# Twelve pairs instead of eight in the first pass of the up products, a new order for two operand sums, and another buffer for one product of the last rows

## The chip, the cores and the metric

The kernel runs on one core of one Trainium2 chip. The metric is the device time of the whole program in microseconds (us). Below, PE is the matrix engine (TensorE), DVE the vector engine, ACT the scalar engine, POOL is GpSimd, and SP is the engine that issues most transfers.

## The reference

A trunk of two layers over 1024 tokens of width 1024, all in float32. Every sub-layer is `h = h + post_norm(sublayer(pre_norm(h)))`. Layer 0 mixes tokens by latent attention, layer 1 by a gated linear recurrence (HGRN2); each is followed by an MLP with 4096 hidden features:

```python
def sq_relu_mlp(h, w1, w2):
    a = jax.nn.relu(h @ w1)
    return (a * a) @ w2

def rms_norm(x, g):
    xf = x.astype(jnp.float32)
    y = xf * lax.rsqrt(jnp.mean(xf * xf, axis=-1, keepdims=True) + EPS)
    return (y * g.astype(jnp.float32)).astype(x.dtype)
```

The change touches the first product of each MLP, `h @ w1` (the up products), and the last normalisation of layer 1's MLP, which ends the kernel.

## The kernel before

**Products in three matmuls.** A float32 operand is split into a high part, rounded by ACT, and a low part, the rest, by DVE (`split`, lines 76 and 77). `mm3` (lines 81 to 83) then makes each product from three matmuls. So every operand, weight or activation, costs one ACT and one DVE instruction before PE can use it, and the split of 128 x 1024 numbers is the common unit.

**Strassen's scheme in the MLP.** The activations A (features by tokens) are seen as 2 x 2 blocks `B11`, `B12`, `B21`, `B22`: the first index halves the features, the second the tokens. B11 and B21 hold the first 512 tokens, B12 (stored whole, unsplit) and B22 the last 512. The weights `w1` are taken in 16 pairs of 128-column blocks (`NP`, the pair's number is `p`). Seven products per pair replace eight. Each product is 12 matmuls of 128 x 512 columns (four feature tiles by three, in `product`), so a pair is 84 matmuls. The right-hand operands are B11, B21, B22 and four sums of blocks, T1 to T4:

- `tsums12` makes T1 and T2, `tsums34` makes T3 and T4. Each T is made in two halves of 128 x 1024 by DVE additions and subtractions and then a split. The temporaries come from the four tiles of tag `s`; the two that `tsums12` leaves in `t2s` are read again for T4.
- All four T need the last rows of tokens. B11 and B21 don't.

**First pass.** For the pairs `p < EARLY` the two products that need only the first 512 tokens are made ahead of everything else, two pairs at a time: `raw_early` loads the pair's first 128 columns (512 KB), `w_parts` splits them, `first_two` multiplies by B11 and ACT copies the sum into `sP1` (line 814), POOL sends `sP1` to `psp` in HBM (line 879), `add_second` adds the product with B21, and ACT makes squared ReLU `h11` of it (lines 806 and 807), which `spill` sends to `hsp` (line 803). `sP1` and `h11` of the first pass live in a ring of two tiles, tag `he`. This pass fills PE while the last token rows are still being normalised, transposed (`into_features`, lines 176 to 181) and summed into T1 to T4. Its instructions are traced with a priority 150 places ahead of their own (`AHEAD`); the transposes of the rows stand 150 (layer 0) or 250 places (layer 1) behind theirs (`LAG`).

**Main pass.** For every pair, `raw_half` loads the pair's two halves of weights (`rA`, `rB`, 512 KB each) into three raw tiles in turn. For `p < EARLY`, `h11` and `sP1` are read back from HBM (lines 894 and 896, SP's queue) and `others` makes the remaining five products. For later pairs all seven products are made there. `others` makes the weight sums `s12` (lines 826, 827) and `s34` (832, 833), splits them (`wS12`, `wS34`), and multiplies: b = wS12 x T2, c = wS12 x T1, d = wS34 x T3, then c += wS34 x B22 and d += wb x T4. DVE adds `U = b + sP1` (837), `X5 = c + U` (844), then `h22`, `h12`, `h21` (848, 851, 854); c gets its second product only after X5 has read it. Four more sums (859 to 869) and seven spills follow.

**What sets the order.** The program is traced in the order of the code, and a list scheduler then fixes each engine's order of instructions at compile time: by priority (place in the trace, shifted as above) among what is ready in its own estimate of times. The tiles of a ring are given out when free. The engines run their fixed orders and wait on semaphores.

**The end of the kernel.** In layer 1's `mlp_down`, `done(t)` finishes each of the last four row tiles: DVE adds the last product (line 1103), ACT squares the sum for the mean (line 135), DVE multiplies the same tile by the gain in place (1105), adds the two means (144), POOL takes the power -0.5 (145), DVE scales and adds the residual (1109), SP stores. `U[t]` is a tile of the same shape whose values are no longer needed there.

Of the kernel before, what the change touches and what calls it, by code (L numbers as in the profile page):

```python
# [16 lines left out]
ALU = mybir.AluOpType  # L17
# [19 lines left out]
ROPE_BASE = 10000.0  # L37
LAG = (150, 100, 250)
AHEAD = (150, 150)
EARLY = 8  # L40
SCALE = (NOPE + ROPE) ** -0.5


# [15 lines left out]
def trunk(ctx, tc, x, x_t, positions, norm_gains, mla_w_in, mla_q_norm, mla_kv_norm, mla_w_uq, mla_w_ukv, mla_w_o,  # L59
          hgrn_w_in, hgrn_lb_logits, hgrn_o_norm, hgrn_w_o, mlp_w1, mlp_w2, out):  # L60
    nc = tc.nc
    PE, ACT, DVE, POOL, SP = nc.tensor, nc.scalar, nc.vector, nc.gpsimd, nc.sync
# [6 lines left out]
    def new(p, shape, dt, tag, bufs=None):  # L69
        uid[0] += 1  # L70
        kw = {} if bufs is None else {"bufs": bufs}
        return p.tile(shape, dt, tag=tag, name=f"{tag}_{uid[0]}", **kw)

    def split(dst, src):

        ACT.activation(dst[:, 0], src, AF.Copy)  # L76
        DVE.tensor_tensor(dst[:, 1], src, dst[:, 0].bitcast(F32), ALU.subtract)  # L77
# [587 lines left out]
    with qstack:  # L665
        with tc.tile_pool(name="mla_wo", bufs=1, side="left", reuse_waits="tile") as wp:
            wv = mla_w_o[0].rearrange("(k p) c -> p k c", p=P)
            ms0 = new(wp, [P, NT], F32, "ms0")
            for n in range(2):
                ws = [wunit(wv[:, 2 * i:2 * i + 2, n * 512:(n + 1) * 512], (2, 512)) for i in range(4)]  # L670
                if n == 0:
                    open_A(True)
                    gpost = row_bcast(wp, "gpost", norm_gains[0, 1], D)
                    gpre = row_bcast(wp, "gpre", norm_gains[0, 2], D)
                for t in range(NT):
# [6 lines left out]
                    y = new(wp, [P, D], F32, "y", 3)  # L682
# [19 lines left out]
    hsp = new(dram, [7, NP * P, 512], F32, "hsp")  # L702
    psp = new(dram, [EARLY * P, 512], F32, "psp")

    def mlp_up(layer):
# [4 lines left out]
        with tc.tile_pool(name=f"up{layer}", bufs=1, side="left", reuse_waits="tile") as wp:  # L710
# [5 lines left out]
            T3 = new(wp, [P, 2, 4, 512], F32R, "T3")  # L716
# [3 lines left out]
            B11, B12, B21, B22 = A[0, 0], A["whole"], A[1, 0], A[1, 1]  # L720
            T1 = A[0, 1] if (0, 1) in A else new(wp, [P, 2, 4, 512], F32R, "T1")

            def f32(x):
                return x.bitcast(F32)


            def tmp():
                return new(wp, [P, 1024], F32, "s", NS).rearrange("p (k c) -> p k c", c=512)

            def part(X, i, k):  # L730
                return f32(X[:, i, k:k + 2])

            def by_tile(x):
                return x.rearrange("p k (t q) -> p k t q", q=P)

            def b12(k):

                return B12[:, :, k:k + 2].rearrange("p t k q -> p k t q")
# [13 lines left out]

            def tsums34():
                for k in (0, 2):
                    e = t2s[k]
                    DVE.tensor_tensor(e, part(B21, 0, k), e, ALU.subtract)
                    DVE.tensor_tensor(e, e, part(B21, 1, k), ALU.add)
                    split(T4[:, :, k:k + 2], e)
                for k in (0, 2):
                    a = tmp()  # L760
                    DVE.tensor_tensor(by_tile(a), by_tile(part(B22, 0, k)), b12(k), ALU.subtract)
                    DVE.tensor_tensor(a, a, part(B22, 1, k), ALU.add)
                    split(T3[:, :, k:k + 2], a)

            def product(ps, w, X, more=False):

# [27 lines left out]
            def w_parts(src):  # L794
                own["w"] = own.get("w", 0) + 1
                w = new(G0, [P, 2, 1024], F32R, "w", 1) if own["w"] % 5 == 0 else new(G, [P, 2, 1024], F32R, "w", 4)
                n = src.shape[1] * src.shape[2]
                v = w[:, :, :n].rearrange("p i (k c) -> p i k c", c=src.shape[2])
                split(v, src)
                return v  # L800
# [23 lines left out]
            def others(p, rA, rB, wb, sP1, h11, second=None, then=None):  # L824
                s12 = new(wp, [P, 1024], F32, "s", NS).rearrange("p (k c) -> p k c", c=256)
                DVE.tensor_tensor(s12[:, :, :P], rA[:, :, P:], rB[:, :, P:], ALU.add)
                DVE.tensor_tensor(s12[:, :, P:], s12[:, :, :P], rA[:, :, :P], ALU.subtract)
                wS12 = w_parts(s12)
                if then is not None:
                    then()  # L830
                s34 = new(wp, [P, 1024], F32, "s", NS).rearrange("p (k c) -> p k c", c=256)
                DVE.tensor_tensor(s34[:, :, :P], rA[:, :, :P], rA[:, :, P:], ALU.subtract)
                DVE.tensor_tensor(s34[:, :, P:], rB[:, :, :P], s12[:, :, P:], ALU.subtract)
                b = new(PG, [P, 512], F32, "tr")
                product(b, wS12[:, :, :, P:], T2)
                U = h512()
                DVE.tensor_tensor(U, b, sP1, ALU.add)
                if second is not None:
                    h11 = second()
                wS34 = w_parts(s34)  # L840
                c = new(PM, [P, 512], F32, "mm")
                product(c, wS12[:, :, :, :P], T1)
                X5 = h512()
                DVE.tensor_tensor(X5, c, U, ALU.add)
                d = new(PM, [P, 512], F32, "c")
                product(d, wS34[:, :, :, :P], T3)
                h22 = h512()
                DVE.tensor_tensor(h22, d, X5, ALU.add)
                product(c, wS34[:, :, :, P:], B22, True)
                h12 = X5  # L850
                DVE.tensor_tensor(h12, c, U, ALU.add)
                product(d, wb, T4, True)
                h21 = U
                DVE.tensor_tensor(h21, d, U, ALU.add)
                for h in (h22, h12, h21):
                    act2(h, h)
                spill(3, p, h22)
                s1 = h512()
                DVE.tensor_tensor(s1, h12, h22, ALU.add)
                spill(4, p, s1)  # L860
                s2 = h512()
                DVE.tensor_tensor(s2, s1, h11, ALU.subtract)
                spill(5, p, s2)
                s3 = h12
                DVE.tensor_tensor(s3, h11, h12, ALU.subtract)  # L865
                spill(6, p, s3)
                spill(1, p, h21)
                s4 = h512()
                DVE.tensor_tensor(s4, h21, s2, ALU.subtract)
                spill(2, p, s4)  # L870

            for p in range(0, EARLY, 2):

# [16 lines left out]
            for p in range(NP):  # L890
# [7 lines left out]
                else:  # L898
                    a, sP1 = first_two(p, w_parts(rA[:, :, :P]))
# [3 lines left out]
    def mlp_down(layer, src, dst, gpre_row):  # L903

        w2 = mlp_w2[layer].rearrange("(q g p) c -> p g q c", g=2, p=P)
        with tc.tile_pool(name=f"down{layer}", bufs=1, side="left", reuse_waits="tile") as wp:
# [36 lines left out]
            for c in range(NC):  # L943
# [74 lines left out]
                if c == 0:  # L1018

                    y = [new(wp, [P, D], F32, f"y{t}") for t in range(4)]  # L1020
                    new(wp, [P, 2, 512], F32, "s21", KC // 2)
                    U = [new(wp, [P, 512], F32, f"u{t}") for t in range(4)]
# [16 lines left out]
                c21, c22 = [v[:, :512] for v in y[4:]], [v[:, 512:] for v in y[4:]]  # L1039
# [8 lines left out]
                if last:  # L1048
# [4 lines left out]
                    gpost = row_bcast(wp, "gpost", norm_gains[layer, 3], D)  # L1053
# [12 lines left out]
                if last:  # L1066
                    gpre = None if gpre_row is None else row_bcast(wp, "gpre", gpre_row, D)
                    for t in range(4):
                        ms12 = meansq(c12[t], new(wp, [P, 512], BF16, "junk"))
                        finish_rows(wp, y[t], [ms11[t], ms12], gpost, gpre, src, dst, t, xt=rows_in("s11", t),  # L1070
                                    part=slice(512, D))
                product(6, X, s22.get, True)
                gather(c22, X, c22)
                if not last:
                    product(3, X, s21.get, True)
                    gather(c21, X)
                elif gpre is not None:
                    sr.close()
                    wr = wp
                    open_A()  # L1080
                    for t in range(4):
                        with tc.high_priority(offset=-LAG[1]):
                            into_features(y[t], act["A"], t)

                    def done(t):
                        DVE.tensor_tensor(c21[t], X[t], c21[t], ALU.add)
                        finish_rows(wp, y[4 + t], None, gpost, gpre, src, dst, 4 + t, xt=xts[t])
                        POOL.dma_start(later[t * P:(t + 1) * P, :], y[4 + t])

                    product(3, X, s21.get, True, n1=2)  # L1090
                    xts = []
                    by_tiles(3, X, s21.get, 2, done, False, lambda: xts.extend(rows_in("s21", 4 + t) for t in range(4)))
                else:
                    s22s, xts = {}, []
                    for t in range(4):

                        s22s[t] = meansq(c22[t], new(wp, [P, 512], BF16, "junk"))
                        DVE.tensor_tensor(c22[t], c22[t], gpost[:, 512:], ALU.mult)

                    def done(t):  # L1100
                        rows = slice((4 + t) * P, (5 + t) * P)
                        xt = xts[t]
                        DVE.tensor_tensor(c21[t], X[t], c21[t], ALU.add)  # L1103
                        ms = meansq(c21[t], new(wp, [P, 512], BF16, "junk"))
                        DVE.tensor_tensor(c21[t], c21[t], gpost[:, :512], ALU.mult)
                        r = rstd_from(ms, s22s[t])
                        for n in range(2):
                            h = slice(n * 512, (n + 1) * 512)
                            DVE.scalar_tensor_tensor(xt[:, h], y[4 + t][:, h], r, xt[:, h], ALU.mult, ALU.add)  # L1109
                            SP.dma_start(dst[rows, h], xt[:, h])  # L1110

                    by_tiles(3, X, s21.get, 0, done, True, lambda: xts.extend(rows_in("s21", 4 + t) for t in range(4)))
                    sr.close()
# [275 lines left out]
```

## Time and profile before

| | |
|---|---|
| median of 3 runs | 2336.49 us (2329.7 to 2338.51) |
| the profiled execution: its own time | 2335.4 us |
| its span, first to last instruction | 2333.7 us |
| ACT busy, share of the span | 1170.1 us, 50% |
| POOL busy, share of the span | 346.1 us, 15% |
| HBM traffic over the span | 142 GB/s |
| granted PE clock, mean | 0.993 |

The profile lists, for each engine, busy time, groups of equal instructions by line, and the idle time in front of an instruction with what ended it (`[2.49 <-DVE w L77]` means: idle for 2.49 us until DVE had finished the tile w at line 77). A table by window gives busy time and the number of instructions (x) of each engine, the PE clock and the DMA rate in a stretch of the span. Layer 0's up products run from about 482 to 815 us of the span, layer 1's from about 1690 to 2022 us. Matmuls overlap in the records, so a row's duration is longer than the distance from one to the next.

### The profile page before, as it was taken

The page shows a single profiled execution, that of the slowest core. Times are in us where ns is not written, and L with a number is a line of the kernel's source. Part 1 is how long each engine was busy: PE and PEld are TensorE (multiplying, and loading weights), DVE is VectorE, ACT ScalarE, POOL GpSimd, SP SyncE. Part 2 cuts the span into 40 slices and gives each one's busy share as a digit, 9 for nine tenths or more (in the row PEclk, how much of TensorE's full clock was granted, in tenths as well). Part 3 has the DMA queues.
Part 4 walks back from the last instruction along what each step waited for, and adds up shares of the span by engine and source line. Part 5 has one row for each costly group of instructions (what it writes and reads, how often), then busy time and mean ns, then how long its engine had stood idle before and what let it go on. Part 6 is the DMA issues. An engine that isn't in the chain of part 4 may idle for free. (4 is left out here: it accounts for less than half of the span.)

```text
span 2333.7 us, 30701 instructions
## 1 busy us (share of the span) xinstructions
PE 2266.3 (97%) x11487; PEld 1912.8 (82%) x11487; DVE 1595.5 (68%) x2287; ACT 1170.1 (50%) x1893; POOL 346.1 (15%) x718
## 2 busy tenths in 40 slices
PE   8999999998999999999999999999989999999998
PEld 8789998876788888888888888888777888888886
DVE  5658886378766557588666667756678776566696
ACT  5436554364444444445565546755464444444443
POOL 1300000021222100001232213312121221100001
PEclk9999999999999999999999999999999999999999
DMA  7010002464654484565612334222355644663664
GB/s 221 23 33 10 10 10 71 145 231 161 219 171 162 167 288 144 180 215 177 207 47 90 101 98 136 79 76 73 95 186 191 222 155 149 222 238 114 223 214 158
DMA packets 229283, 333.12 MB, mean 143 GB/s; under 512 B 16743, under 2 KB 136590, under 8 KB 229134
## 3 DMA queue, kind: packets, MB, share of 16 engines
q1 hardware_dynamic: 205326, 251.45, 33.4%
q0 software_dynamic: 23808, 79.71, 9.3%
q8 instruction: 90, 1.47, 0.3%
q14 instruction: 59, 0.48, 0.1%
HBM read 247.22 MB, written 83.89 MB: 142 GB/s over the span
## 5 line engine op out<-in xcount | busy, mean ns | idle before, releaser
L77 DVE TENSOR_TENSOR w<-raw,w 128x1024 fp32r<-128x1024 f32 (+1 forms) x240 | 278.1, 1164 | 165.4 <-ACT w L76 164.6
L76 ACT ACTIVATE w<-raw 128x1024 fp32r<-128x1024 f32 (+1 forms) x240 | 237.8, 996 | 211.6 <-PE mm L83 82.4
L81 PE MATMUL mm<-A,w 128*128 128x512 f32 x832 | 329.6, 397 | 6.8 <-ACT he L814 2.9
L82 PE MATMUL mm<-A,w 128*128 128x512 f32 x832 | 327.4, 394 | 0.6 <-DVE A L77 0.6
L83 PE MATMUL mm<-A,w 128*128 128x512 f32 x832 | 325.7, 393 | 0.0
L76 ACT ACTIVATE w<-s 128x1024 fp32r<-128x1024 f32 x156 | 164.8, 1059 | 312.0 <-PE tr L83 120.5
L77 DVE TENSOR_TENSOR w<-s,w 128x1024 fp32r<-128x1024 f32 x156 | 190.2, 1221 | 140.8 <-ACT w L76 140.3
L81 PEld LDWEIGHTS mm<-A,w 128*128 128x128 f32 x832 | 157.5, 189 | 43.2 <-ACT he L814 4.0
L145 POOL TENSOR_TENSOR rstd<-rstd,nhalf 128x1 f32<-128x1 f32 x56 | 44.4, 794 | 965.5 <-DVE rstd L144 939.0
L83 PEld LDWEIGHTS mm<-A,w 128*128 128x128 f32 x832 | 157.3, 189 | 32.9
L82 PEld LDWEIGHTS mm<-A,w 128*128 128x128 f32 x832 | 157.4, 189 | 32.5 <-DVE A L77 1.0
L82 PE MATMUL mm<-w,w 128*128 128x512 f32 x432 | 168.6, 390 | 0.7 <-DVE w L77 0.7
L83 PE MATMUL mm<-w,w 128*128 128x512 f32 x432 | 168.3, 390 | 0.0
L81 PE MATMUL mm<-w,w 128*128 128x512 f32 x432 | 154.2, 391 | 0.8 <-DVE y L1036 0.4
L803 POOL DMA_DIRECT2D hsp<-h x176 | 94.8, 540 | 349.0 <-ACT h L807 176.8
L81 PE MATMUL mm<-w,A 128*128 128x256 f32 (+2 forms) x352 | 111.8, 320 | 4.3 <-ACT A L76 3.5
L83 PE MATMUL mm<-w,A 128*128 128x256 f32 (+2 forms) x352 | 111.3, 318 | 0.0
L82 PE MATMUL mm<-w,A 128*128 128x256 f32 (+2 forms) x352 | 110.6, 316 | 0.0
L83 PE MATMUL c<-T,w 128*128 128x512 f32 x256 | 99.4, 391 | 4.4 <-DVE w L77 4.4
L81 PE MATMUL c<-T,w 128*128 128x512 f32 x256 | 100.3, 392 | 1.6 <-ACT w L76 1.6
L82 PE MATMUL c<-T,w 128*128 128x512 f32 x256 | 99.7, 389 | 0.0
L81 PEld LDWEIGHTS mm<-w,w 128*128 128x128 f32 x432 | 81.0, 188 | 19.2 <-ACT u L1034 0.8
(441 smaller groups left out, 5648.4 us busy)
## 6 DMA issues: line engine op xcount, KB each, us to landing
raw<-in_mlp_w_dram SPq DMA_DIRECT2D x92, 512.0 KB, 5.0
hsp<-h POOLq DMA_DIRECT2D x176, 256.0 KB, 3.2
s<-in_mlp_w_dram SPq DMA_DIRECT2D x80, 512.0 KB, 5.9
raw<-hsp SPq DMA_DIRECT2D x76, 512.0 KB, 3.9
raw<-in_hgrn_w_in_dram SPq DMA_DIRECT2D x64, 512.0 KB, 4.2
sx<-hsp SPq DMA_DIRECT2D x36, 512.0 KB, 4.0
hsp<-he POOLq DMA_DIRECT2D x48, 256.0 KB, 3.3
xt<-in_x_dram SPq DMA_DIRECT2D x16, 512.0 KB, 6.1
```

What stands on the lines that cost most here:

```text
L76: ACT.activation(dst[:, 0], src, AF.Copy)
L77: DVE.tensor_tensor(dst[:, 1], src, dst[:, 0].bitcast(F32), ALU.subtract)
L81: PE.matmul(ps, lhs[0], rhs[0], start=start, stop=False, skip_group_check=more)
L82: PE.matmul(ps, lhs[0], rhs[1], start=False, stop=False, skip_group_check=more)
L83: PE.matmul(ps, lhs[1], rhs[0], start=False, stop=stop, skip_group_check=more)
L145: POOL.tensor_tensor(r, r, nhalf[:, :1], ALU.pow)
L803: POOL.dma_start(hsp[i, p * P:(p + 1) * P, :], h)
```

## The change

Four edits. `EARLY` goes from 8 to 12: pairs 8 to 11 of both layers move their first two products into the first pass, with `psp` sized to match. In `tsums34` the two halves of T3 are traced ahead of the two of T4. In `others` of pair 0, `tsums34` (called through `rest` and `then`) is traced behind the sums `s34` and their split `wS34` instead of ahead of them. In `done`, the gain's product goes to `U[t]` instead of back to `c21[t]`, and the last step reads it there.

```diff
-EARLY = 8
+EARLY = 12
...
             def tsums34():
                 for k in (0, 2):
+                    a = tmp()
+                    DVE.tensor_tensor(by_tile(a), by_tile(part(B22, 0, k)), b12(k), ALU.subtract)
+                    DVE.tensor_tensor(a, a, part(B22, 1, k), ALU.add)
+                    split(T3[:, :, k:k + 2], a)
+                for k in (0, 2):
                     e = t2s[k]
                     DVE.tensor_tensor(e, part(B21, 0, k), e, ALU.subtract)
                     DVE.tensor_tensor(e, e, part(B21, 1, k), ALU.add)
                     split(T4[:, :, k:k + 2], e)
-                for k in (0, 2):
-                    a = tmp()
-                    DVE.tensor_tensor(by_tile(a), by_tile(part(B22, 0, k)), b12(k), ALU.subtract)
-                    DVE.tensor_tensor(a, a, part(B22, 1, k), ALU.add)
-                    split(T3[:, :, k:k + 2], a)
...
                 wS12 = w_parts(s12)
-                if then is not None:
-                    then()
                 s34 = new(wp, [P, 1024], F32, "s", NS).rearrange("p (k c) -> p k c", c=256)
...
                 wS34 = w_parts(s34)
+                if then is not None:
+                    then()
                 c = new(PM, [P, 512], F32, "mm")
...
-                        DVE.tensor_tensor(c21[t], c21[t], gpost[:, :512], ALU.mult)
+
+                        DVE.tensor_tensor(U[t], c21[t], gpost[:, :512], ALU.mult)
                         r = rstd_from(ms, s22s[t])
-                        for n in range(2):
+                        for n, z in ((0, U[t]), (1, c22[t])):
                             h = slice(n * 512, (n + 1) * 512)
-                            DVE.scalar_tensor_tensor(xt[:, h], y[4 + t][:, h], r, xt[:, h], ALU.mult, ALU.add)
+                            DVE.scalar_tensor_tensor(xt[:, h], z, r, xt[:, h], ALU.mult, ALU.add)
                             SP.dma_start(dst[rows, h], xt[:, h])
```

## The prediction

> **What bounds the kernel now.** I read the page's first rows, then the busy table by windows, then PE's timeline at the two places that table points to.
>
> ```profile
> span 2333.7 us, 30701 instructions
> PE 2266.3 (97%) x11487; PEld 1912.8 (82%) x11487; DVE 1595.5 (68%) x2287; ACT 1170.1 (50%) x1893; POOL 346.1 (15%) x718
> ```
>
> PE is busy in 2266.3 of 2333.7 us, and the change alters no matmul. So it can win only where PE stands still or runs slowly, and what lies outside the span (2335.4 - 2333.7 = 1.7 us) stays.
>
> ```profile
> 533.00:557.00 24.00, 17.03 (x54) 12.33 (x53) 21.85 (x25) 9.77 (x12) 0.57 (x2) 0.79 0.35 112
> 575.00:600.00 25.00, 21.76 (x94) 17.05 (x93) 17.26 (x25) 10.10 (x16) 3.78 (x7) 1.00 0.62 201
> 600.00:620.00 20.00, 20.00 (x90) 16.54 (x89) 17.90 (x27) 10.59 (x17) 6.44 (x12) 1.00 0.66 223
> 680.00:760.00 80.00, 80.00 (x355) 66.25 (x354) 51.88 (x73) 38.69 (x55) 16.70 (x31) 1.00 0.49 163
> 1740.00:1763.00 23.00, 13.88 (x41) 9.81 (x40) 22.96 (x26) 9.18 (x11) 0.54 (x1) 0.78 0.27 92
> 1763.00:1800.00 37.00, 34.46 (x151) 27.85 (x150) 28.96 (x42) 15.42 (x22) 6.45 (x12) 1.00 0.61 201
> ```
>
> The columns are the stretch, its length, busy time and count of PE, PEld, DVE, ACT and POOL, then the PE clock, DMA share and GB/s. From 680 to 760 PE runs without a break: 80.00 / 355 = 0.2254 us per matmul. The first row holds 54 matmuls, 12.2 us of work in 24 us: **11.8 lost**. The row at 1740 holds 41, 9.2 us in 23: **13.8 lost**. In both DVE is busy almost throughout (21.85 of 24, 22.96 of 23). Right behind them another 25 - 94 x 0.2254 = 3.8 and 37 - 151 x 0.2254 = 3.0 us go. These 32.4 us are what the first three edits can reach.
>
> ```profile
> 535.19 0.50 PE L81 MATMUL tr<-T,w 128*128 128x512 f32 x1 [1.63 <-ACT w L76]
> 538.89 0.80 PE L83 MATMUL tr<-T,w 128*128 128x512 f32 x1 [2.49 <-DVE w L77]
> 546.86 0.50 PE L81 MATMUL c<-T,w 128*128 128x512 f32 x1 [0.67 <-ACT w L76]
> 549.78 0.50 PE L83 MATMUL c<-T,w 128*128 128x512 f32 x1 [2.18 <-DVE w L77]
> 1743.87 0.50 PE L81 MATMUL tr<-T,w 128*128 128x512 f32 x1 [3.48 <-ACT w L76]
> 1747.63 0.79 PE L83 MATMUL tr<-T,w 128*128 128x512 f32 x1 [2.56 <-DVE w L77]
> ```
>
> These are the first products with T operands. Each waits for a split: the two at `tr` for wS12 (tile b), the two at `c` for wS34 (tile d). PE has emptied the first pass at 535.19 - 1.63 = 533.6 and at 1743.87 - 3.48 = 1740.4, ahead of the operands. Idle time isn't all of the loss:
>
> ```profile
> 537.32:544.14 6.82, 5.25 (x12) 4.13 (x13) 6.82 (x7) 1.06 (x1) 0.00 (x0) 0.50 0.21 62
> 550.97:554.38 3.41, 3.41 (x9) 2.64 (x9) 3.38 (x5) 0.48 (x1) 0.00 (x0) 0.50 0.02 5
> ```
>
> Behind the gaps the granted clock is 0.50, for 6.82 and for 3.41 us. PE's busy time there runs at half speed: (5.25 + 3.41) / 2 = 4.3 of the 11.8 us. The Trainium skill, "TensorE: Matmul & The Clock Gate", section "Why this matters for your kernels", asks only that no PE gap exceed about 3 us. By that rule the gaps of 1.63 to 2.49 us above would have cost no clock; the trace disagrees, and by the rule removing them would bring 4.3 us less in layer 0.
>
> **The four added pairs.** A pair's two products are 24 matmuls, 24 x 0.2254 = 5.4 us; four pairs carry PE 21.6 us further, to 533.6 + 21.6 = 555.2 and 1740.4 + 21.6 = 1762.0. The same matmuls leave the main pass, so PE's sum stays. Does everything late now come in time?
>
> ```profile
> 517.52 1.23 DVE L745 TENSOR_TENSOR s<-whole,A 128x1024 f32<-128x1024 f32 x1 [1.83 <-ACT whole L178]
> 537.62 1.22 DVE L77 TENSOR_TENSOR w<-s,w 128x1024 fp32r<-128x1024 f32 x1
> 550.84 1.21 DVE L77 TENSOR_TENSOR T<-s,T 128x1024 fp32r<-128x1024 f32 x1
> 1726.26 1.23 DVE L745 TENSOR_TENSOR s<-acc,A 128x1024 f32<-128x1024 f32 x1 [3.17 <-ACT acc L178]
> 1746.36 1.22 DVE L77 TENSOR_TENSOR w<-s,w 128x1024 fp32r<-128x1024 f32 x1
> 1759.59 1.21 DVE L77 TENSOR_TENSOR T<-s,T 128x1024 fp32r<-128x1024 f32 x1
> ```
>
> These are the first sum, the split of wS12 and the last split of a T, per layer. DVE works through them from 517.5 to 552.1 and from 1726.3 to 1760.8. The added pairs put four 1024-wide splits (1.22 us each) ahead: 4.9 us. wS12 then ends at 538.8 + 4.9 = 543.7 and 1747.6 + 4.9 = 1752.5, against PE's need at 555.2 and 1762.0. The last T ends at 557.0 and 1765.7; with T3 first that is T4, needed four products of 2.7 us later, at 566.0 and 1772.8. T3, 7.3 us of DVE earlier (six instructions), is wanted after two products, at 560.6 and 1767.4. So the first pass covers the sums with about 7 us to spare or more, and all **25.6 us** go. The two **order edits** I put at 0 (bounds: 0 and, should T3 in layer 1 slip behind 1767.4, one gap like the 2.18): the longer pass hides either order, and wS34 no longer waits behind the sums.
>
> **What the added pairs cost.** ACT gets per pair the split and three copies:
>
> ```profile
> L807 ACT ACTIVATE he<-he 128x512 f32<-128x512 f32 x3 | 1.9, 634 | 0.1
> L806 ACT ACTIVATE he<-mm 128x512 f32<-128x512 f32 x3 | 1.8, 600 | 4.6 <-PE mm L83 4.6
> L814 ACT ACTIVATE he<-mm 128x512 f32<-128x512 f32 x2 | 1.2, 599 | 1.2 <-PE mm L83 1.2
> 1713.59 0.60 ACT L814 ACTIVATE he<-mm 128x512 f32<-128x512 f32 x1 [3.03 <-DMA hsp<-he]
> 1714.09 1.05 ACT L76 ACTIVATE w<-raw 128x1024 fp32r<-128x1024 f32 x1
> L81 PE MATMUL mm<-A,w 128*128 128x512 f32 x832 | 329.6, 397 | 6.8 <-ACT he L814 2.9 <-DVE h L844 1.3 <-ACT w L76 1.1
> ```
>
> 1.05 + 0.60 + 0.60 + 0.63 = 2.9 us in 5.4 us of PE: hidden. The risk is the ring of two `he` tiles: line 814 at 1713.59 stood 3.03 us for a spill, with the weight split of 1714.09 and all ACT work queued behind it. PE's idle time for line 814 is 2.9 us over both layers' sixteen pairs (last row), 0.2 a pair: 8 x 0.2 = **1.6** (bounds 0 and 3.0, the wait itself, once in each layer: 6.1).
>
> Next late, now that the operands aren't, is the ring's round trip for pair 0, whose `h11` and `sP1` take the same two tiles:
>
> ```profile
> 535.95 0.54 POOL L803 DMA_DIRECT2D hsp<-he  x1 [2.92 <-ACT he L807]
> 538.45 0.34 SPq L896 DMA_DIRECT2D he<-psp  x1
> he<-psp SPq DMA_DIRECT2D x5, 256.0 KB, 2.7
> 1744.63 0.54 POOL L803 DMA_DIRECT2D hsp<-he  x1 [4.77 <-ACT he L807]
> ```
>
> The last spill starts 2.35 us after the pass ends (533.6); SP waits and issues the reading back of sP1 at +4.85; it takes 2.7; U and X5 take 0.68 each: +8.9. PE wants X5 done after three products, at +8.1: 0.8 us late. In layer 1 the spill came at +4.2, which gives 2.7 us late, but ACT then stood for a T split that now comes earlier. Bounds: 0, if another product fills in, and 2.7 plus half of 3.41 us of clock, 4.4. I take 1.0 a layer, near layer 0's row: **2.0**.
>
> In the main pass pairs 8 to 11 now read `h11` and `sP1` back, as pairs 0 to 7 do:
>
> ```profile
>   DMA hsp<-h: 5.5, 2
>   DMA h<-psp: 3.8, 3
> ```
>
> (idle time of DVE ahead of line 837, U.) In its order stand the splits PE needs. The sixteen such pairs of before lost 3.8 + 3.0 = 6.8 us outside the two gaps, 0.43 each: 8 x 0.43 = **3.4** (bounds: 0, as in the row 600 to 620, where two such pairs run with PE at 20.00 of 20, and 3.8 each, as at 575). Each added pair moves 1.25 MB more (its 512 KB load and three transfers of 256 KB): 10 MB, hidden, since the row at 600 holds 223 GB/s with PE full; DMA queues to PE as at 575 are the price without that cover.
>
> **The last rows.**
>
> ```profile
> 2324.94 0.69 DVE L1103 TENSOR_TENSOR y<-c,y 128x512 f32<-128x512 f32 x1 [0.99 <-PE c L83]
> 2326.26 0.19 ACT L135 ACTIVATION_READ_ACCUMULATOR junk<-y 128x1 f32 x1
> 2326.48 0.69 DVE L1105 TENSOR_TENSOR y<-y,gpost 128x512 f32<-128x512 f32 x1 [0.85 <-ACT junk L135]
> 2327.09 0.15 DVE L144 SCALAR_TENSOR_TENSOR rstd<-ssq,ssq 128x1 f32<-128x1 f32 x1
> ```
>
> Line 1105 overwrites what ACT reads, so it waits for ACT and delays line 144. Into `U[t]` it runs at 2325.6, beside ACT, and 144 follows ACT at 2326.48: 2327.09 - 2326.48 = **0.6** at the very end, where nothing hides it.
>
> **Sum.** 25.6 + 0.6 - 1.6 - 2.0 - 3.4 = 19.2 us. 2335.4 - 19.2 = 2316.2 on the profiled execution, 2336.5 - 19.2 = **2317.3** on the median, 1.1 above it. I forecast 2317.
>
> **The rivals.**
>
> *More than the sum.* The sums end before the pass does, so pair 0 and 1 start with their weights split, and the 6.8 us behind the gaps vanish with the backlog of DVE: no 3.4, no 2.0. That gives 25.6 + 0.6 + 6.8 = 33.0, 2303; half of it, 2310. For it: DVE at 575 was working off what the gap had left. Against: the waits at 837 are for transfers.
>
> *The last rows are held back (about no change).* The first sum needs the last row's transposes, and these rank behind the early pairs.
>
> ```profile
> 1717.59 1.28 DVE L205 SCALAR_TENSOR_TENSOR acc<-xt,rstd,gpre 128x1024 f32<-128x1024 f32 x1 [0.74 <-POOL rstd L145]
> 1725.64 0.59 ACT L178 ACTIVATE acc<-tr 128x512 f32<-128x512 f32 x1
> ```
>
> The row was ready at 1718.9, its transposes copied at 1725.6: 6.8 us behind early products. If the four new pairs went ahead too, the sums would start up to 21.6 us later and PE would meet the same gaps: 2336.5 - 0.6 + 1.6 = 2337; in one layer only, 2337 - 13 = 2324. Against: pairs 8 to 11 are traced last of the pass, and the transposes found their place with three pairs still to go.
>
> *The added pairs stall in the main pass (slower).* Each of the eight waits for its reading back as at 575 to 600: 3.8 us and half of one 3.41 us clock window, 5.5. 8 x 5.5 = 44: 2336.5 - 26.2 + 44 = 2354. It decides from 26.2 / 8 = 3.3 us a pair. For it: 837's waits. Against: the row at 600.
>
> *The order edits do nothing*, because the scheduler places by readiness: the same 2317, by the slack above.
>
> **Chances.** Forecast (2310 to 2325) 0.58; more than the sum 0.17; held back 0.18; stalls 0.07. A measurement of this kernel can tell about 0.5%, 11.7 us, from no change. So faster 0.75, same 0.18, slower 0.07. The range 2306 to 2333 leaves out the stalls, the held-back case in both layers and the top of the second.
>
> **What would show it.** Right: early products until about 555 and 1762; no gap over 1 us and no clock of 0.50 there, first T products without an idle wait for w; DVE's first sum still near 517 and 1726; line 1105 beside ACT's 135. Wrong: first sums 10 us later or more (held back); idle PE ahead of tiles b and c in pairs 8 to 11, with 837 waiting for `h<-psp` (stalls); a gap of 2 us or more ahead of c's second product (the ring mis-sized).

## The result and the profile after

| | before | after |
|---|---|---|
| median | 2336.21 us (4 runs, 2329.7 to 2338.51) | 2316.35 us (4 runs, 2313.2 to 2319.12) |
| the profiled execution: its own time | 2335.4 us | 2313.2 us |
| its span | 2333.7 us | 2311.5 us |

The ratio of the medians is 0.9925, 95% interval 0.9911 to 0.9939: 2336.21 - 2316.35 = 19.9 us gone, where the prediction's sum was 19.2. The two profiled executions differ by more, 22.2 us; that of after is the fastest of its four.

The profile after, the first rows of the page:

```profile
span 2311.5 us, 30767 instructions
PE 2259.8 (98%) x11487; PEld 1910.7 (83%) x11487; DVE 1597.4 (69%) x2287; ACT 1167.1 (50%) x1892; POOL 346.9 (15%) x726
```

The matmuls are the same 11487. PE's busy time fell by 2266.3 - 2259.8 = 6.5 us, mostly work that no longer runs at half clock, and its idle time from 67.4 to 2311.5 - 2259.8 = 51.7, by 15.7. Together that is the 22.2 us. Where they went shows in the table by windows of after, in the columns of the prediction's first such table, at the same two places:

```profile
533.00:557.00 24.00, 24.00 (x107) 19.89 (x106) 22.18 (x24) 14.78 (x22) 4.34 (x8) 1.00 0.56 184
557.00:575.00 18.00, 18.00 (x81) 14.88 (x81) 11.00 (x15) 5.82 (x9) 1.63 (x3) 1.00 0.51 149
575.00:600.00 25.00, 22.68 (x98) 17.80 (x97) 20.12 (x29) 11.08 (x16) 5.95 (x11) 1.00 0.77 265
1727.00:1762.00 35.00, 33.77 (x149) 27.62 (x148) 29.21 (x33) 19.32 (x28) 5.55 (x11) 1.00 0.55 179
1762.00:1790.00 28.00, 25.59 (x113) 20.86 (x112) 20.37 (x29) 10.59 (x15) 3.79 (x7) 1.00 0.61 199
```

From 533 to 557 PE now starts 107 matmuls where it started 54, at full clock, beside a DVE that is as busy as before (22.18 us against 21.85): the work of DVE is the same, but PE has something to do meanwhile. What is left: 25 - 98 x 0.2254 = 2.9 us, 35 - 149 x 0.2254 = 1.4 and 28 - 113 x 0.2254 = 2.5.

To see the whole span, the next table sums, over all matmuls of a part, the distance from one start to the next less the median distance of such a matmul in before (so gaps and half clock both count). Up 0 and up 1 are the up products of layers 0 and 1, down 0 and down 1 the second products of their MLPs. Down 0 and the HGRN stand together, since 24 matmuls changed places between them.

```
lost us                      before   after
ahead of the up products       18.9    18.4
up 0: first + main pass  6.7 + 15.6    6.4 + 2.9
down 0 and the HGRN            37.2    39.1
up 1: first + main pass  6.3 + 13.5    4.9 + 4.9
down 1                          0.8     0.3
last matmul's start to end      9.2     9.2
```

The up products lose 42.1 us before and 19.0 after: 23.1 gained. The main passes have it nearly all (29.1 to 7.8). In before, the waits of 1.63 and 3.48 us ahead of the first T products are counted in the first passes.

### The profile page after: what moved, and what is told of

It is laid out like the page before. It is cut to its first block, busy times and chain, and to the rows that moved or that the text cites. A ratio compares the mean times of both kernels' runs of the same rounds, so it can differ in the third digit from the quotient of the medians.

```text
span 2311.5 us, 30767 instructions
## 1 busy us (share of the span) xinstructions
PE 2259.8 (98%) x11487; PEld 1910.7 (83%) x11487; DVE 1597.4 (69%) x2287; ACT 1167.1 (50%) x1892; POOL 346.9 (15%) x726
## 5 line engine op out<-in xcount | busy, mean ns | idle before, releaser
L806 ACT ACTIVATE h<-h 128x512 f32<-128x512 f32 x80 | 50.0, 626 | 98.7 <-DVE h L848 73.0
```

The lines of the kernel that those rows point to most:

```text
L806: ACT.activation(h, src, AF.Relu)
```

## Experiments

The theory: the change wins by `EARLY` alone, because four more pairs of early products cover DVE's work on the T sums; what is left in the up products is mostly the ring of two `he` tiles; the two order edits do nothing; and the gain on the last rows is taken back by something behind them. Rivals: the order edits have a share in it; the reading back of the added pairs is what is left; or more early pairs would bring more.

### One: each part of the change alone

`EARLY = 12` in before, nothing else:

```diff
-EARLY = 8
+EARLY = 12
```

> Before with twelve pairs in the first pass and nothing else of the change (T4's sums traced first, in front of s34 and wS34; the gain's product in place). Cover theory: the longer first pass alone hides the sums, so nearly the whole gain stays, 2316 to 2319 us, and the first products with T operands show no idle time ahead of them. Rival, the order edits carry a share: the gaps ahead of tile d (0.67 and 2.18 us, with half of a 3.41 us clock window, about 4.5 us a layer) come back, 2325 us.

Measured: 2313.91 us (4 runs) against 2333.89 (13 runs), 0.9911 (0.9895 to 0.9928). The interval overlaps that of the whole change, 0.9911 to 0.9939. This one number carries the result.

The two order edits alone, with eight pairs (the part of the diff in `tsums34` and in `others`):

```diff
 def tsums34():            # T3's halves ahead of T4's
...
-                if then is not None:
-                    then()
...                        # behind s34 and its split
+                if then is not None:
+                    then()
```

> Before with the two order edits alone, eight pairs in the first pass. Cover theory: PE still empties the first pass near 533.6 and 1740.4, so the gaps ahead of tile b stay; at most the gaps ahead of tile d (about 4.5 us a layer) go, 2327 to 2337 us. Slot theory: T3's sums need a temporary of the ring s while T4's are made in place, so DVE still does T4 before T3, and the time is that of before, 2336 us or a little over. Rival, the edits do what they say and carry the change: T3 runs first and 2320 us or less.

Measured: 2333.61 us (10 runs) against 2333.89, 0.9999 (0.9989 to 1.0008): nothing. PE's timeline in this kernel, rows with idle time ahead of a T product in layer 0:

```profile
532.15 0.50 PE L81 MATMUL tr<-T,w 128*128 128x512 f32 x1 [1.77 <-ACT w L76]
534.85 0.79 PE L83 MATMUL tr<-T,w 128*128 128x512 f32 x1 [1.50 <-DVE w L77]
545.69 0.50 PE L81 MATMUL c<-T,w 128*128 128x512 f32 x1 [3.16 <-ACT T L76]
547.77 0.79 PE L81 MATMUL tr<-T,w 128*128 128x512 f32 x1 [1.58 <-ACT w L76]
```

The edit does what it says: at `c`, PE no longer waits for the split of wS34 but for that of a T. And it brings nothing, since DVE is no less full. The table by windows of this kernel, at the same place as before's 21.85 of 24:

```profile
533.00:557.00 24.00, 17.76 (x57) 13.41 (x56) 21.75 (x25) 7.96 (x9) 0.46 (x1) 0.79 0.34 111
```

57 matmuls instead of 54. Nor did the order that the edit writes come out. DVE's timeline in after (761 and 762 are T4's lines now, 756 and 757 T3's):

```profile
531.12 1.22 DVE L761 TENSOR_TENSOR s<-A,s 128x1024 f32<-128x1024 f32 x1
533.59 1.22 DVE L762 TENSOR_TENSOR s<-s,A 128x1024 f32<-128x1024 f32 x1
542.16 1.22 DVE L756 TENSOR_TENSOR s<-A,whole 128x1024 f32<-128x1024 f32 x1
545.03 1.22 DVE L757 TENSOR_TENSOR s<-s,A 128x1024 f32<-128x1024 f32 x1
```

T4 still comes first, and T3 11 us later, although it is traced first. A likely reason, from the code: T4 is summed in place in `t2s`, while T3 needs a new tile of the four `s`, of which `t2s` holds two and s12 and s34 take the others.

The last rows alone, with eight pairs:

```diff
-                        DVE.tensor_tensor(c21[t], c21[t], gpost[:, :512], ALU.mult)
+                        DVE.tensor_tensor(U[t], c21[t], gpost[:, :512], ALU.mult)
```

> Before with the gain's product of the last rows into the other buffer alone. The time can't tell 0.6 us; the trace can. Prediction's step: line 144 comes 2.0 us after the last matmul starts instead of 2.6, and the span ends 8.6 us after it instead of 9.2. Rival, seen in the trace of after, where line 144 came 0.6 us earlier and the span still ended 9.2 us after the last matmul: POOL's closing drain sets the end, and it stays 9.2.

One execution: 2333.5 us. At the end itself the edit shows: from the start of the last matmul to the end of the span it is 8.59 us here and 9.18 in before, the 0.6 that was forecast. With twelve pairs the edit wins the same 0.6: it is 9.84 us in the kernel with `EARLY` alone and 9.23 in after. What makes both longer than with eight pairs is told in five.

### Two: how many pairs

After, with `EARLY = 10` and with `EARLY = 16`.

> The changed kernel with ten pairs in the first pass instead of twelve. Cover theory: the pass ends 10.8 us later than before, near 544 and 1751; wS12 is ready by then, the last of T3 or T4 is not by the third product, so the gaps ahead of b are gone and up to 3 us a layer may stay ahead of d: 2317 to 2323 us. Rival, the gain goes by the number of pairs, half of 20 us: 2326 us.

Measured: 2323.21 us (4 runs) against 2333.89, 0.9956 (0.9939 to 0.9973): about half the gain of twelve. PE's timeline, rows with idle time:

```profile
567.83 0.50 PE L83 MATMUL tr<-T,w 128*128 128x512 f32 x1 [1.22 <-DVE w L77]
573.81 0.50 PE L81 MATMUL c<-T,w 128*128 128x512 f32 x1 [1.15 <-ACT w L76]
577.25 0.79 PE L81 MATMUL mm<-A,w 128*128 128x512 f32 x1 [2.71 <-DVE he L844]
1754.75 0.80 PE L81 MATMUL tr<-T,w 128*128 128x512 f32 x1 [2.37 <-ACT w L76]
```

Waits for splits of w are back ahead of T products (the three shown, and 0.85 us at 552.70 and 1.87 at 1775.97), none longer than 2.37 us, where before's longest is 3.48. The wait at 577.25 is for an X5 whose U waited 4.80 us for a sum read back (`h<-psp`, DVE at 575.78). The time alone can't tell the two expectations apart, since half the gain also fits a gain by the number of pairs; the waits and the next kernel do. Ten pairs don't quite cover DVE's work, twelve do.

> The changed kernel with all sixteen pairs in the first pass. Nothing is left to cover, so what is seen is the price of eight more pairs that go through HBM. Forecast's price, 0.43 us a pair for the reading back and 0.2 for the ring he: 8 x 0.63 = 5 us over the changed kernel, 2321 us. Stall theory, 3.8 to 5.5 us a pair: 30 to 44 us over, 2346 to 2360 us. Rival, the price is nothing: 2316 us.

Measured: 2329.06 us (10 runs) against 2332.73 (16 runs), 0.9986 (0.9974 to 0.9998), so nearly all of the gain is lost again. Not in the up products: these lose 22.1 us, 3.1 more than after, 0.39 for each of the eight pairs that it has more than after. It is the step to layer 0's down products. PE's and ACT's timelines there:

```profile
828.50 0.79 PE L81 MATMUL mm<-w,w 128*128 128x512 f32 x1 [4.32 <-ACT u L1034]
```

```profile
815.34 2.01 ACT L76 ACTIVATE w<-raw 128x1024 fp32r<-128x1024 f32 x2 [6.38 <-DMA raw<-hsp]
817.26 1.04 ACT L76 ACTIVATE w<-sx 128x1024 fp32r<-128x1024 f32 x1
823.17 1.06 ACT L76 ACTIVATE w<-s 128x1024 fp32r<-128x1024 f32 x1 [4.87 <-DMA s<-in_mlp_w_dram]
826.91 1.06 ACT L76 ACTIVATE w<-raw 128x1024 fp32r<-128x1024 f32 x1 [2.68 <-DMA raw<-hsp]
827.87 1.07 ACT L1034 ACTIVATE u<-mm 128x512 f32<-128x512 f32 x2
```

ACT stands 6.38, 4.87 and 2.68 us for loads ahead of weight splits (line 76), with the copies `u` for which PE waits queued behind. From 820 to 840 the table by windows shows the DMA engines busy throughout (share 1.00, the last number but one):

```profile
820.00:840.00 20.00, 15.68 (x59) 12.45 (x58) 7.06 (x6) 7.96 (x10) 0.00 (x0) 0.83 1.00 364
```

20 - 59 x 0.2254 = 6.7 us go there. Another 1.0 of the 14.0 us between the two spans stands at the end of the kernel (10.25 us after the last matmul's start, against 9.23). So the reading back within the up products isn't the main price of more pairs; loads that come late at the next stage are. Full DMA engines aren't enough to explain it: in after, from 805 to 825, the DMA share is 0.98 at 351 GB/s and PE is full. What differs is when the loads are issued: SP issues the first `s<-in_mlp_w_dram` at 818.10 here and at 807.12 in after, though the down products begin within 1 us of each other (796.8 and 796.0), and from 815 to 820 the DMA share is only 0.30. Why the loads come late is open: the traces show it, and no kernel isolates it.

### Three: the ring for pair 0

After, with the tiles of pair 0's `h11` and `sP1` taken from the `h` ring first, so that they don't wait for the first pass's spills:

```diff
-            ring = ["he"] * 2 + ["h"] * NH + ["h2"] * NM
+            ring = ["h"] * NH + ["he"] * 2 + ["h2"] * NM
```

What it is to remove, in after, layer 1: PE's, SP's and DVE's timelines.

```profile
1768.65 0.50 PE L81 MATMUL mm<-A,w 128*128 128x512 f32 x1 [2.41 <-DVE h L844]
```

```profile
1763.77 0.34 SPq L896 DMA_DIRECT2D he<-psp  x1
```

```profile
1767.18 0.69 DVE L835 TENSOR_TENSOR h<-tr,he 128x512 f32<-128x512 f32 x1 [2.82 <-DMA he<-psp]
1767.91 0.69 DVE L844 TENSOR_TENSOR h<-mm,h 128x512 f32<-128x512 f32 x1
```

SP issues the load of pair 0's sP1 at 1763.77, U (line 835 here) waits for it, X5 (844) follows, and PE stands 2.41 us ahead of the product that X5 frees: the gap ahead of c's second product that the prediction had priced.

> The changed kernel with the main pass's ring of tiles begun at the tag h instead of he, so that pair 0's h11 and sP1 don't wait for the last spills of the first pass. Ring theory: the idle 2.41 us of PE ahead of c's second product in layer 1 (1768.65 in the trace of after) is the round trip through the two he tiles, and goes; 2314 us. Rival, X5 is late for another reason: the gap stays at 2 us or more, 2316 us.

Measured: 2308.49 us (4 runs) against 2332.73, 0.9897 (0.9883 to 0.9912). DVE's and PE's timelines and the table by windows:

```profile
1759.91 0.69 DVE L844 TENSOR_TENSOR he<-mm,he 128x512 f32<-128x512 f32 x1
```

```profile
1761.80 0.39 PE L81 MATMUL mm<-A,w 128*128 128x512 f32 x1
```

```profile
565.00:600.00 35.00, 35.00 (x156) 28.99 (x155) 27.09 (x41) 15.72 (x24) 8.62 (x16) 1.00 0.66 220
1727.00:1762.00 35.00, 35.00 (x156) 29.00 (x155) 28.43 (x34) 16.30 (x25) 5.11 (x10) 1.00 0.55 180
1762.00:1790.00 28.00, 28.00 (x125) 23.19 (x124) 22.63 (x33) 14.94 (x23) 6.47 (x12) 1.00 0.59 196
```

X5 now ends at 1759.91 + 0.69 = 1760.60, 1.2 us before PE takes up the product that it frees, at 1761.80 and without a wait; and PE is full in all three stretches. The up products lose 14.9 us instead of 19.0. That is more than the 2.41: the losses from 575 to 600 in layer 0 went too. There PE waits in after 0.40 us for an X5 in a tile `he` (586.61) and 1.15 and 0.78 us for splits of weights (593.53, 595.51); the last two stand, within 0.01 us, in each of the four kernels with twelve pairs whose ring begins at `he`, and in neither of the two whose ring begins at `h`. How they hang on the ring isn't settled. Of the 5.8 us between the two spans, 1.4 stand in the part ahead of the up products, which the edit doesn't touch, and are taken for scatter. The interval of the ratio just meets after's (0.9911 to 0.9939).

### Four: T3 early by force

In before, with eight pairs, T3's sums traced right behind T1's and T2's, ahead of pair 0's s12, so that T3 finds its tile free:

```diff
+            def tsums3():         # T3's loop, out of tsums34
...
             tsums12()
+            tsums3()
```

> Before (eight pairs) with T3's sums traced right behind T1's and T2's, ahead of pair 0's s12, so that they get their temporaries first. Slot theory: DVE now does do T3 early, ahead of wS12, and since wS12 is what PE waits for first, the gap ahead of tile b grows by up to T3's 7.3 us a layer while that ahead of d shrinks: 2336 to 2346 us. Rival, only the sum of DVE's work counts: 2336 us. Rival, T3 early is a gain by itself: under 2330 us.

Measured: 2338.35 us (7 runs) against 2332.73, 1.0029 (1.0017 to 1.0041), slower. T3 does come early: its first sum is line 763 here. DVE's and PE's timelines:

```profile
525.27 1.22 DVE L763 TENSOR_TENSOR s<-A,whole 128x1024 f32<-128x1024 f32 x1
544.83 2.35 DVE L77 TENSOR_TENSOR w<-s,w 128x1024 fp32r<-128x1024 f32 x2
```

```profile
544.53 0.80 PE L81 MATMUL tr<-T,w 128*128 128x512 f32 x1 [14.18 <-ACT w L76]
1758.40 0.80 PE L81 MATMUL tr<-T,w 128*128 128x512 f32 x1 [15.92 <-ACT w L76]
```

So a place in the trace decides only when the tile is free too, which fits the reason given above. And the order alone wins nothing: the several gaps become one, of 14.18 and 15.92 us, and the up products lose 24.3 and 20.0 us in the two layers, against 22.3 and 19.8 in before. DVE has the same work ahead of the T products in either order.

### Five: the end of the kernel

The last rows' multiplication runs in after as forecast. DVE's and ACT's timelines:

```profile
2302.66 0.69 DVE L1103 TENSOR_TENSOR y<-c,y 128x512 f32<-128x512 f32 x1 [1.59 <-PE c L83]
2303.39 0.69 DVE L1106 TENSOR_TENSOR u<-y,gpost 128x512 f32<-128x512 f32 x1
2304.20 0.16 DVE L144 SCALAR_TENSOR_TENSOR rstd<-ssq,ssq 128x1 f32<-128x1 f32 x1
```

```profile
2303.98 0.19 ACT L135 ACTIVATION_READ_ACCUMULATOR junk<-y 128x1 f32 x1
```

The product into `u` (line 1106) runs beside ACT, and line 144 follows ACT's 135 at once: 2304.20 - 2302.24 = 1.97 us after the last matmul's start (2302.235), where before it was 2327.09 - 2324.52 = 2.57. Yet the span ends 9.23 us after that matmul, not 8.59. What stands at the end is POOL. The view of the program's last line gives the closing instructions of each engine as count, durations in ns (least, median, longest), and first and last start; before, then the kernel with the last rows alone, then after:

```profile
L1385 POOLq DRAIN  x3: 40/93/5566, 2327.4 to 2333.4; - x3
```

```profile
L1386 POOLq DRAIN  x3: 40/102/5566, 2325.5 to 2331.5; - x3
```

```profile
L1386 POOLq DRAIN  x3: 40/93/6221, 2304.5 to 2311.2; - x3
L1386 POOLq EVENT_SEMAPHORE  x4: 17/17/17, 2310.7 to 2311.4; - x4
```

The first DRAIN starts with POOL's last power (line 145), lasts 6.22 us, and the closing semaphores follow at its end, 2310.7. It lasted 5.57 with eight pairs. POOL issues 272 transfers before and 280 after (the counts of the DMA view on POOL's queue; the spills of sP1 make the difference):

```profile
psp<-he POOLq DMA_DIRECT2D x16, 256.0 KB, 2.7
```

```profile
psp<-he POOLq DMA_DIRECT2D x24, 256.0 KB, 3.1
```

The first is before, the second after. 0.65 us for 8 transfers is 0.082 each. If that is the cause, then taking POOL's transfers away must shorten it, and letting POOL end earlier must bring its end forward.

After, with the 24 transfers to `psp` issued by SP:

```diff
-                        POOL.dma_start(psp[i * P:(i + 1) * P, :], sP1)
+                        SP.dma_start(psp[i * P:(i + 1) * P, :], sP1)
```

> The changed kernel with the 24 transfers of sP1 to psp issued by SP instead of POOL. Drain theory: POOL's closing drain grows by 0.081 us for each transfer that POOL issued (5.57 us at 272 in the trace of before and of tail8, 5.89 at 276 in early10, 6.22 at 280 in after, 6.87 at 288 in early16), so with 256 it takes 4.3 us and the span ends 7.5 us or less after the last matmul's start. Rival, it goes by the pairs of the first pass or by the length of the program: 6.2 us and 9.2 us again. On the time: SP keeps its order, so a load queued behind such a transfer waits for ACT's copy; the first pass may lose a few us.

One execution: 2308.9 us. That is more below after than the end explains, and a single execution can't settle why.

```profile
L1386 POOLq DRAIN  x3: 40/102/4261, 2301.8 to 2306.9; - x3
```

256 transfers, 4.26 us, and the span ends 7.60 us after the last matmul's start instead of 9.23 (7.5 or less was expected). The other kernels lie on the same line: 5.89 us at 276 (ten pairs), 6.87 at 288 (sixteen). From 256 to 288 that is (6.87 - 4.26) / 32 = 0.082 us a transfer.

After, with the last tile's factor made by ACT and DVE, so that POOL has nothing to do there (the square root's table is loaded by a square root of the tile before):

```diff
+                        if t == 3:
+                            ACT.activation(small("ssq", 8, 8)[:, :1], r2[0], AF.Sqrt)
...
+                            r = small("rstd", 8, 8)[:, :1]
+                            DVE.scalar_tensor_tensor(r, ms, EPS, s22s[t], ALU.add, ALU.add)
+                            ACT.activation(r, r, AF.Sqrt)
+                            DVE.reciprocal(r, r)
```

> The changed kernel with POOL's power of the last row tile made by a square root on ACT (its table loaded ahead) and a reciprocal on DVE, so POOL has nothing to do behind the third row. Drain theory: POOL's closing drain ends some 7 us after its last instruction began and sets the end of the span; without that instruction the end moves up from 9.2 us after the last matmul's start to what SP's stores allow, 7.5 us or less. Rival, the end is set by something counted from the last matmul: 9.2 us again.

One execution: 2313.28 us, span 2311.6, about after's. At the end itself:

```profile
L1395 POOLq DRAIN  x3: 40/102/6222, 2301.0 to 2311.3; - x3
```

The DRAIN is as long as in after (280 transfers in both) but starts at 2301.0, 3.2 us before the last matmul (2304.23), and is over by 2307.3. The span then ends 7.33 us after that matmul, 1.9 earlier than in after. That this doesn't show in the total comes from other parts: the main pass of layer 1 alone loses 7.1 us here and 4.9 in after, with the same edits there. PE's wait for X5 is 2.69 us here, and 3.41 us at half clock follow it from 1768.52 on; in after's 2.41 none did (the last section says why).

### Six: both that helped

After with the ring of three and the tail of five.

> The changed kernel with both finds together: the main pass's ring begun at h, and POOL left out of the last row tile's power. Ring and drain theories: the gains add, about 5 us for the ring and 1.9 us for the end (7.3 us after the last matmul's start instead of 9.2): 2306 us, ratio 0.989 or less to the kernel before. Rival, the ring's gain was chance of the fixed orders: 2313 us.

Measured: 2306.96 us (4 runs, 2306.18 to 2308.0) against 2335.99 (7 runs), 0.988 (0.9863 to 0.9896). Its interval lies wholly below that of after. It is the best kernel of these runs, though its interval overlaps that of the ring alone: the 1.9 us at the end are seen in the trace, not in the time. Its span ends 7.50 us after the last matmul, and from 565 to 600 and from 1727 to 1790 PE is full as in the ring's kernel. With SP issuing `psp` besides, it wasn't run.

## Why the prediction was right, and where it wasn't

**The sum, 19.2 against 19.9: right, with some luck.** The up products were to win 25.6 - 1.6 - 2.0 - 3.4 = 18.6 us and won 23.1 in the profiled pair. One term was too dear by about 5 us and another gave nothing, as below, and the profiled execution of after is the fastest of its four.

**The lost 25.6 us go: right.** The windows at both places are full and at full clock, and `EARLY` alone gives the whole result. The times at which the early products end were read too rigidly. The first T product starts at 547.97 and 1744.32, and early ones still follow it (their last copies start at 559.50 and 1756.31): the scheduler mixes the two. And the 1762 of layer 1 should have been lowered by the 11.8 us that layer 0 had already won.

**The order edits cost nothing: right.** The covering pass was given as the reason; with eight pairs the edits bring nothing either, since DVE's total work is the limit there. The rival "the scheduler places by readiness" holds as far as tiles are concerned: T3 stayed behind T4. So the step that put T4's split last was wrong: the last is T3's. It did no harm, since that split ends at 553.66 + 1.23 = 554.9 in layer 0, and PE takes up T3's product at 561.57.

**The `he` ring in the first pass, 1.6: right.** PE's idle time for line 814 is 4.3 us in after and was 2.9, so 1.4. The page's row of after:

```profile
L81 PE MATMUL mm<-A,w 128*128 128x512 f32 x832 | 329.6, 397 | 9.4 <-ACT he L814 4.3
```

**The ring's round trip for pair 0, 1.0 in each layer: the sum right, the layers not.** 2.41 us in layer 1, inside the 2.7 that was worked out for it, and none in layer 0. By the prediction's own sign (a gap of 2 us or more ahead of c's second product) the term was mis-sized there; that the two layers together come near 2.0 is luck.

**Reading back pairs 8 to 11, 3.4: too dear.** The main passes of after lose 2.9 + 4.9 = 7.8 us, less the 2.41 of the round trip 5.4, for 24 pairs that read back. The forecast was 6.8 for the old sixteen and 3.4 for the eight, 10.2. The error is in the 0.43 a pair: it was taken from losses that weren't all the reading back's. Before's PE stood 2.37 us until 589.18 for a U, and DVE came late to this U since it had itself stood 2.40 us for a load of weights (`s<-raw,raw`, line 826, at 584.13). With the other ring the same 24 pairs read back, and the main passes lose only 2.6 us. So the rival "more than the sum" came about in this term, though its reason, a backlog of DVE left by the gap, isn't what that wait shows; the kernel with the other ring is where its 2303 to 2310 was reached.

**The added transfers are hidden: wrong in one place, the last rows' 0.6 with it.** The edit to the last rows gave its 0.6 us, and with the eight added POOL transfers the closing DRAIN took 0.65 back. In the prediction, DMA could cost only by its bytes, in the main pass. The term 0.6 - 0 measured -0.05.

**Not in the sum:** down 0 and the HGRN lost 1.8 us more in the profiled pair. The edits don't touch these parts; with unchanged `EARLY` they lost 37.2 to 39.1 in the traces of the four kernels with eight pairs, so 39.1 in after is taken for scatter.

**The rivals that fell.** The last rows weren't held back: DVE's timeline of after has the first sums at

```profile
513.75 1.23 DVE L745 TENSOR_TENSOR s<-whole,A 128x1024 f32<-128x1024 f32 x1 [0.16 <-ACT whole L178]
1711.66 1.23 DVE L745 TENSOR_TENSOR s<-acc,A 128x1024 f32<-128x1024 f32 x1 [2.89 <-ACT acc L178]
```

which is 3.8 and, with layer 0's gain taken off, 2.8 us earlier than before (517.52 and 1726.26 - 11.8), not later. The stalls of 5.5 us a pair did not come either: from twelve pairs to sixteen, each further one cost 0.39 in the up products.

## What to carry to other kernels

Where PE waits for a full vector engine, look for other PE work to put there, and count how much: with ten pairs the gaps came back, with twelve they were gone at the first T products, with sixteen the next stage paid. A new order of instructions won nothing here while the engine behind the wait was busy throughout, and what is traced first isn't first if its tile isn't free. What a step adds has to be counted at the end of the kernel too, by engine: there a few transfers took back what another edit had won.

## What the runs showed of the hardware

**POOL's closing DRAIN grew with the transfers that POOL issued**: 4.26 us at 256, 5.57 at 272, 5.89 at 276, 6.22 at 280, 6.87 at 288, and the same to 0.01 us in the four traces with 272 and the five with 280. That is 0.082 us for each further transfer to `psp`, the only kind whose number these kernels change. The line doesn't pass through zero (256 x 0.082 would be 21 us), so what other transfers add isn't shown. The DRAIN starts with POOL's last computing instruction (2304.48 and 2304.51 in after), so work of POOL in the last microseconds puts all of it at the end of the span.

**A gap's length alone doesn't tell whether the clock is halved.** In after the gap of 2.41 us at 1768.65 left the granted clock at 1.00 (the row 1762 to 1790 above). A gap of 2.34 us in the kernel with `EARLY` alone and one of 2.37 with ten pairs each came with half clock. PE's row for the first, and the windows around both:

```profile
1769.00 0.57 PE L81 MATMUL mm<-A,w 128*128 128x512 f32 x1 [2.34 <-DVE h L844]
```

```profile
1766.00:1774.00 8.00, 5.66 (x18) 4.20 (x18) 5.04 (x8) 2.67 (x4) 0.54 (x1) 0.79 0.21 58
```

```profile
1752.00:1760.00 8.00, 5.51 (x18) 3.92 (x17) 7.04 (x9) 3.08 (x3) 0.00 (x0) 0.79 0.23 65
```

A mean of 0.79 over 8 us is 3.4 us at half clock ((1 - 0.79) x 8 / 0.5). The Trainium skill, "TensorE: Matmul & The Clock Gate", section "Why this matters for your kernels", would have none of the three cost clock; two did.

These traces show what decides: where the gap lies. In each trace the clock changes only at whole multiples of 3.413 us from one another (the half-clock stretches of before start at 537.32, 550.97, 1745.63 and 1759.29: 4, 354 and 358 such steps from the first). These steps divide the span into stretches of 3.41 us. After's gap is shared between two of them, and PE is busy for 2.39 and 2.02 us in these; with `EARLY` alone it lies whole in one, 1765.88 to 1769.29, where PE is busy for 1.07, and the next is at half clock; with ten pairs PE is busy for 1.49 us in the stretch ahead of the half clock. Over all twelve traces (the first 10 and last 8 us left out), each of the 61 stretches at full clock that were followed by half clock had PE idle for 1.67 us or more, and none of the 7931 others for more than 1.92. The steps lie differently in each trace, so one and the same gap may cost clock in one execution and not in another.
